# GpSimd's queue takes the stores and fetches of the split weights; SyncE's queue keeps the other transfers

## The chip, the core and the metric

The kernel runs on one core of a Trainium2 chip. A core has five engines that run their own instruction streams in order: TensorE (PE in the profile, with its weight loads shown apart as PEld), VectorE (DVE), ScalarE (ACT), GpSimd (POOL) and SyncE (SP). Transfers between the chip's memory (DRAM) and the core's on-chip memory are carried by 16 DMA engines; a transfer is started by an instruction on the queue of some engine, and an instruction that has to wait for something holds back all that stand behind it on that queue. The metric is the device time of one execution in microseconds; lower is better. A difference of about 0.3% is what a measurement of this kernel can tell from no change.

## What is computed

One inference step of a one-layer hybrid decoder trunk in float32, for a prompt of 2048 tokens and 8 single-token samples, with width 1024:

```python
h = rmsnorm(x, norm_mix)
p = h @ w_in                                  # 1024 x 3980, one combined projection
y_a = gdn_mixer(p_a, ...)                     # gated DeltaNet, chunks of 64
y_b = rwkv_mixer(p_b, ...)                    # RWKV-7
y_c = hgrn_mixer(p_c, ...)                    # HGRN2
x = x + concat(y_a, y_b, y_c) @ w_out         # 1024 x 1024
h = rmsnorm(x, norm_ffn)
u = silu(h @ w_gate) * (h @ w_up)             # 1024 x 2816, twice
x = x + u @ w_down                            # 2816 x 1024
y = rmsnorm(x, norm_final)
```

Beside `y` for prompt and samples, the new states of the three mixers are returned.

## The kernel before, in words

Activations lie transposed: 128 partitions are 128 channels, the free axis is time. Time is cut into four quarters of 512 columns; the last has 520, since the 8 samples are appended, and is worked on as two pieces of 260. For each quarter the kernel does the input projection (31 tiles of 128 output channels, `proj`), the mixers ("units" of two heads, `gdn`, `rwkv`, `hgrn`), the output projection (`out_proj`) and the feed-forward part (`ffn`). A driver (`Driver`, `emit`) writes the units' vector work out between the big products, and a scheduler then fixes the order of every engine's instructions by a model of their times; all of that is settled when the program is built.

Every big product is made exact enough by splitting both operands in two float32r parts, hi and lo, and adding three matmuls: hi·hi, hi·lo, lo·hi (L377, L378, L379, in `mm3`). `load_w` supplies the weights, 512 columns ("a half" of a weight tile of 1024) at a time:

- In the first quarter (q = 0) it loads the raw weight (L331, 256 KB), ACT copies it to hi (L332), DVE makes lo = raw − hi (L333), and the two parts, side by side in one tile `hl`, are stored to DRAM (L340, 512 KB).
- In the quarters after it the two parts are fetched back into such a tile (L347, 512 KB).
- Once the mixers are through, `late` is set and the tiles come from the mixers' buffers; hi and lo are then fetched apart (L345, 256 KB each), up to four weight tiles ahead (`stream`, `AHEAD`). The store at L338 is the same for a late first quarter, which does not occur.

There are four `hl` tiles. So a fetch waits until PE has ended with the half that was fetched four halves earlier, and a split in the first quarter waits until the older store from that tile has landed. The raw weights have three buffers for `w_in` (names `rw_in`) and two for the others (`rw_o`, `rw_wg`, `rw_wu`, `rw_wd`). In the trace, `w_in`, `w_o`, `w_wg`, `w_wu`, `w_wd` are the `hl` tiles, `sw_...` their copies in DRAM, and `hw_...`, `lw_...` the late parts.

Nearly all transfers are issued from SyncE's queue, in the scheduler's order: the weights, the x pieces (`raw_x`, L405), the projected rows (`s_p`, stored at L485 and L489, read back at L497), the mixers' inverses through DRAM (L666 to L694), their results (`s_mix`, L759, read back as `mxs`, L529), the residual (`res`, L537) and the outputs. GpSimd has some 40 instructions in all, among them a few memsets at the start, 20 memsets of the few columns that lie before the first quarter's rows (L496, in `slice_p`), 8 memsets of a whole tile in the HGRN units (`att_h`, L1216) and 6 products at the very end (L643). A memset waits until the buffer it writes is free.

Of the kernel before, what the change touches and what calls it, by code (L numbers as in the profile page):

```python
# [91 lines left out]
class Kern:  # L92
# [218 lines left out]
    def load_w(self, src, key, q, n=1024):  # L311


        nc = self.nc
        out = []
        name = "w_" + "_".join(str(k) for k in key) + f"_{q}"
        for i in range(n // 512):
            if self.late:
                hi, lo = (self.T(f"{j}{name}") for j in "hl")
                parts = hi, lo  # L320
            else:
                hl = self.wp.tile([128, 2, 512], F32, tag="hl", name=name, bufs=4)
                hi, lo = parts = hl[:, 0], hl[:, 1]
            hi, lo = hi.bitcast(F32R), lo.bitcast(F32R)
            if q == 0:
                if key[0] == "in":
                    raw = self.R(f"r{name}")[:, 0:512]
                else:
                    raw = self.wp.tile([128, 512], F32, tag="raw", name=f"r{name}", bufs=2)
                with ExitStack() if key[0] == "in" else self.tc.issue_after(self.mark.ins):  # L330
                    nc.sync.dma_start(raw, src[:, 512 * i:512 * i + 512])  # L331
                nc.scalar.activation(hi, raw, AF.Copy)  # L332
                nc.vector.tensor_tensor(lo, raw, hi, ALU.subtract)  # L333
                kept = self.tc.dram_tile([128, 2, 512], F32, name=f"s{name}_{i}")
                self.kept[key, i] = kept
                if self.late:
                    for j in range(2):
                        nc.sync.dma_start(kept[:, j], parts[j])  # L338
                else:
                    nc.sync.dma_start(kept, hl)  # L340
            else:
                kept = self.kept[key, i]
                if self.late:
                    for j in range(2):
                        nc.sync.dma_start(parts[j], kept[:, j])  # L345
                else:
                    nc.sync.dma_start(hl, kept)  # L347
            out.append((hi, lo))
        return out

# [1348 lines left out]
```

## Time and profile before

| | |
|---|---|
| median of 3 runs | 3178.42 us (3172.18 to 3183.83) |
| profiled execution: its own time | 3181.53 us |
| its span, first to last instruction | 3179.7 us |
| mean granted TensorE clock | 0.979 of full speed |
| DVE busy | 2198.8 us (69%) |
| ACT busy | 1197.5 us (38%) |
| POOL busy | 12.5 us (0%) |
| DMA queue of SyncE | 622.93 MB, 61.4% of the 16 DMA engines' span |
| DMA queue of ACT | 1.07 MB, 0.1% |

"Busy" is the time in which an engine works on an instruction; issuing a transfer is not counted as busy. Matmuls are pipelined and their ends are modelled, so that a PE shown as busy need not be at its peak. A wait is put down to what came last by the profile.

### The profile page before, as it was taken

The page shows a single profiled execution, that of the slowest core. Times are in us where ns is not written, and L with a number is a line of the kernel's source. Part 1 is how long each engine was busy: PE and PEld are TensorE (multiplying, and loading weights), DVE is VectorE, ACT ScalarE, POOL GpSimd, SP SyncE. Part 2 cuts the span into 40 slices and gives each one's busy share as a digit, 9 for nine tenths or more (in the row PEclk, how much of TensorE's full clock was granted, in tenths as well). Part 3 has the DMA queues.
Part 4 walks back from the last instruction along what each step waited for, and adds up shares of the span by engine and source line. Part 5 has one row for each costly group of instructions (what it writes and reads, how often), then busy time and mean ns, then how long its engine had stood idle before and what let it go on. Part 6 is the DMA issues. An engine that isn't in the chain of part 4 may idle for free.

```text
span 3179.7 us, 62651 instructions
## 1 busy us (share of the span) xinstructions
PE 3063.7 (96%) x24812; PEld 2445.6 (77%) x24812; DVE 2198.8 (69%) x5424; ACT 1197.5 (38%) x2063; POOL 12.5 (0%) x41
## 2 busy tenths in 40 slices
PE   7999999999998999999999999997999999999998
PEld 5777777778996677767767777775677777999998
DVE  6783676677667878878788688888676674443334
ACT  5442252244225544553445343546342322221002
POOL 0000000000000000000000000000000000000000
PEclk9999999999999999999999999997999999999999
DMA  8887567657766577676765445555454447755552
GB/s 284 282 287 236 176 194 218 197 175 217 206 179 204 191 240 232 219 232 217 255 188 166 157 158 172 174 181 154 153 170 150 155 158 247 257 170 186 190 182 91
DMA packets 387938, 628.00 MB, mean 198 GB/s; under 512 B 172540, under 2 KB 176892, under 8 KB 387644
## 3 DMA queue, kind: packets, MB, share of 16 engines
q1 hardware_dynamic: 386556, 622.93, 61.4%
q8 instruction: 195, 3.19, 0.4%
q10 hardware_dynamic: 1088, 1.07, 0.1%
q14 instruction: 99, 0.81, 0.1%
HBM read 456.77 MB, written 167.14 MB: 196 GB/s over the span
## 4 chain that ended last, share of the span: by engine, by line
PE 72%; DVE 12%; DMA 9%; ACT 4%; issue 2%; SPq 2%; DVEq 0%; ACTq 0%
PE psp L377 5%; PE psp L378 5%; PE psp L379 5%; PE pd L377 5%; PE pd L379 5%; PE pfu L377 5%; PE pd L378 5%; PE pfu L379 5%; PE pfg L377 4%; PE pfu L378 4%; PE pfg L378 4%; PE pfg L379 4%; DMA rw_in<-w 2%; PE pso L379 1%; PE pso L378 1%
## 5 line engine op out<-in xcount | busy, mean ns | idle before, releaser
L377 PE MATMUL psp<-xs,w_in 128*128 128x512 f32 (+1 forms) x1240 | 447.2, 361 | 21.6 <-ACT xs L417 8.9
L378 PE MATMUL psp<-xs,w_in 128*128 128x512 f32 (+1 forms) x1240 | 443.6, 358 | 0.8 <-DVE xs L418 0.8
L379 PE MATMUL psp<-xs,w_in 128*128 128x512 f32 (+1 forms) x1240 | 438.9, 355 | 0.1
L377 PEld LDWEIGHTS psp<-xs,w_in 128*128 128x128 f32 x1240 | 235.2, 190 | 67.8 <-ACT w_in L332 10.3
L378 PEld LDWEIGHTS psp<-xs,w_in 128*128 128x128 f32 x1240 | 235.2, 190 | 35.6 <-DVE xs L418 2.0
L379 PEld LDWEIGHTS psp<-xs,w_in 128*128 128x128 f32 x1240 | 234.7, 189 | 36.1 <-issue 1.3
L606 DVE TENSOR_TENSOR x<-pd,x 128x512 f32<-128x512 f32 (+1 forms) x240 | 138.2, 583 | 109.9 <-PE pd L379 108.2
L377 PE MATMUL pd<-u,w_wd 128*128 128x512 f32 x496 | 202.0, 414 | 10.0 <-DVE x L606 6.7
L378 PE MATMUL pfg<-xhs,w_wg 128*128 128x512 f32 x496 | 202.6, 408 | 3.7 <-DVE xhs L564 3.6
L377 PE MATMUL pfg<-xhs,w_wg 128*128 128x512 f32 x496 | 202.0, 407 | 0.2
L377 PE MATMUL pfu<-xhs,w_wu 128*128 128x512 f32 x496 | 200.5, 404 | 0.5 <-ACT w_wu L332 0.5
L378 PE MATMUL pd<-u,w_wd 128*128 128x512 f32 x496 | 200.4, 405 | 0.0
L379 PE MATMUL pd<-u,w_wd 128*128 128x512 f32 x496 | 199.1, 403 | 0.0
L379 PE MATMUL pfg<-xhs,w_wg 128*128 128x512 f32 x496 | 199.1, 401 | 0.0
L379 PE MATMUL pfu<-xhs,w_wu 128*128 128x512 f32 x496 | 198.9, 401 | 0.0
L378 PE MATMUL pfu<-xhs,w_wu 128*128 128x512 f32 x496 | 198.3, 400 | 0.0
L585 ACT ACTIVATE t<-t 128x512 f32<-128x512 f32 (+1 forms) x110 | 60.0, 546 | 298.0 <-DVE t L584 292.4
L285 ACT ACT_TABLE_LOAD x91 | 116.8, 1283 | 113.1 <-PE pny L512 23.8
L482 DVE TENSOR_TENSOR p<-psp,ri 128x512 f32<-128x512 f32 (+1 forms) x155 | 89.8, 580 | 72.7 <-PE psp L379 71.3
L362 ACT ACTIVATE u<-t 128x512 fp32r<-128x512 f32 (+1 forms) x110 | 60.1, 546 | 210.7 <-DVE t L588 210.5
L377 PEld LDWEIGHTS pd<-u,w_wd 128*128 128x128 f32 x496 | 94.2, 191 | 34.9 <-DVE x L606 3.0
L587 DVE SCALAR_TENSOR_TENSOR t<-pfu,rf 128x512 f32<-128x512 f32 (+1 forms) x110 | 64.1, 583 | 77.8 <-PE pfu L379 74.7
(645 smaller groups left out, 7296.7 us busy)
## 6 DMA issues: line engine op xcount, KB each, us to landing
w_in<-sw_in SPq DMA_DIRECT2D x186, 512.0 KB, 4.2
w_wg<-sw_wg SPq DMA_DIRECT2D x80, 512.0 KB, 3.3
w_wu<-sw_wu SPq DMA_DIRECT2D x80, 512.0 KB, 3.3
w_wd<-sw_wd SPq DMA_DIRECT2D x80, 512.0 KB, 3.8
sw_in<-w_in SPq DMA_DIRECT2D x62, 512.0 KB, 4.4
s_p<-p SPq DMA_DIRECT2D x93, 256.0 KB, 4.0
sw_wg<-w_wg SPq DMA_DIRECT2D x44, 512.0 KB, 2.9
sw_wu<-w_wu SPq DMA_DIRECT2D x44, 512.0 KB, 2.9
```

What stands on the lines that cost most here:

```text
L285: p = self.nc.scalar.preload_act_table_set("natural_log_exp_and_others")
L362: nc.scalar.activation(out[:, 0], src, AF.Copy)
L377: nc.tensor.matmul(ps, lhsT=hi[:, ws], rhs=xs[:, 0, xc], start=start, stop=False)
L378: nc.tensor.matmul(ps, lhsT=hi[:, ws], rhs=xs[:, 1, xc], start=False, stop=False)
L379: nc.tensor.matmul(ps, lhsT=lo[:, ws], rhs=xs[:, 0, xc], start=False, stop=stop)
L482: nc.vector.tensor_tensor(p[:, c0:c0 + cn], ps, rstd[q][:, c0:c0 + cn], ALU.mult)
L585: nc.scalar.activation(t, g, AF.Tanh, scale=0.5)
L587: nc.vector.scalar_tensor_tensor(p, psu, 0.5, r[:, cs], ALU.mult, ALU.mult)
L606: nc.vector.tensor_tensor(x2[d][:, c0:c0 + cn], ps, x2[d][:, c0:c0 + cn], ALU.add)
```

## The change

Four instructions of `load_w`, which stores and fetches the split weights, are issued from GpSimd's queue and no longer from SyncE's. The raw loads (L331) and every other transfer stay on SyncE.

```diff
                 if self.late:
                     for j in range(2):
-                        nc.sync.dma_start(kept[:, j], parts[j])
+                        nc.gpsimd.dma_start(kept[:, j], parts[j])
                 else:
-                    nc.sync.dma_start(kept, hl)
+                    nc.gpsimd.dma_start(kept, hl)
             else:
                 kept = self.kept[key, i]
                 if self.late:
                     for j in range(2):
-                        nc.sync.dma_start(parts[j], kept[:, j])
+                        nc.gpsimd.dma_start(parts[j], kept[:, j])
                 else:
-                    nc.sync.dma_start(hl, kept)
+                    nc.gpsimd.dma_start(hl, kept)
```

In the built program 1012 transfers change queue: 210 stores (L340), 458 fetches of 512 KB (L347) and 344 late fetches of 256 KB (L345). The scheduler places everything anew, so the order on the other engines shifts by some instructions as well.

SyncE's queue at the program's start, before (`sw_in_0_0` and `sw_in_0_1` are the stores of the first weight tile's halves):

```order
L405 DMA raw_x_229<-xT 128x512 x2
L340 DMA sw_in_0_0_214<-w_in_0_209 128x1024
L340 DMA sw_in_0_1_221<-w_in_0_216 128x1024
L405 DMA raw_x_232<-xT 128x512 x2
L331 DMA rw_in_0_285<-w 128x512
L331 DMA rw_in_0_292<-w 128x512
L186 DMA cst<-cst 128x352
```

The same place on SyncE's queue in the changed program:

```order
L405 DMA raw_x_229<-xT 128x512 x2
L405 DMA raw_x_232<-xT 128x512 x2
L331 DMA rw_in_0_285<-w 128x512
L331 DMA rw_in_0_292<-w 128x512
L186 DMA cst<-cst 128x352
```

The two stores, which wait for DVE's split of the first weight, no longer stand ahead of the last two x pieces and of the next raw weights.

GpSimd's queue in the second quarter's input projection, before (memsets alone):

```order
L496 MEMSET p_g_3741 128x3
L496 MEMSET p_g_3930 128x3
L496 MEMSET pkr_4695 128x1
L496 MEMSET prr_4836 128x1
L496 MEMSET pvr_4852 128x1
```

And in the changed program, from the 105th of the weight transfers on:

```order
L347 DMA w_in_1_4703<-sw_in_0_0_1920 128x1024
L496 MEMSET p_g_3930 128x3
L347 DMA w_in_1_4705<-sw_in_0_1_1927 128x1024
L496 MEMSET pkr_4695 128x1
L347 DMA w_in_1_4777<-sw_in_0_0_2038 128x1024
L347 DMA w_in_1_4779<-sw_in_0_1_2045 128x1024
L347 DMA w_in_1_4904<-sw_in_0_0_2135 128x1024
L496 MEMSET prr_4836 128x1
L347 DMA w_in_1_4906<-sw_in_0_1_2142 128x1024
```

The memsets now have weight fetches ahead of them and behind them on one queue; a memset that waits for its buffer holds the fetches behind it.

## Rows read from the trace of the kernel before

**Rows 1.** The page's first part: busy time of an engine, its share of the span, and the number of instructions.

```profile
PE 3063.7 (96%) x24812; PEld 2445.6 (77%) x24812; DVE 2198.8 (69%) x5424; ACT 1197.5 (38%) x2063; POOL 12.5 (0%) x41
```

**Rows 2.** Busy time by stretch (us from the span's start: length, then the busy time and instructions of PE, PEld, DVE, ACT and POOL; the last three columns are the granted TensorE clock, the busy share of the DMA engines and GB/s).

```profile
0.00:200.00 200.00, 174.26 (x1012) 130.32 (x1013) 152.14 (x336) 103.65 (x168) 2.41 (x20) 0.96 0.87 283
300.00:600.00 300.00, 299.26 (x2564) 221.42 (x2563) 195.45 (x517) 97.89 (x161) 1.13 (x7) 1.00 0.64 198
1000.00:1600.00 600.00, 574.93 (x4325) 429.44 (x4323) 483.15 (x1129) 294.15 (x486) 1.05 (x2) 0.98 0.71 229
2000.00:2200.00 200.00, 184.04 (x1455) 137.97 (x1452) 170.24 (x400) 106.68 (x181) 0.00 (x0) 0.94 0.57 171
2800.00:3000.00 200.00, 200.00 (x1673) 200.00 (x1673) 76.07 (x182) 23.95 (x56) 0.00 (x0) 1.00 0.56 182
```

**Rows 3.** What PE waited for, over the whole span: us in total, times, longest us.

```profile
PE psp L377 <- ACT xs L417: 8.9, 2, 8.7
PE psp L377 <- ACT w_in L332: 8.6, 4, 3.2
...
PE pfu L377 <- DVE x L548: 2.8, 1, 2.8
PE psp L377 <- DMA w_in<-sw_in: 2.8, 3, 1.2
```

**Rows 4.** What SyncE's queue (SPq) waited for, over the whole span: us in total, times, longest us.

```profile
SPq L347 <- PE psp L379: 248.1, 106, 8.4
SPq L347 <- PE pfg L379: 185.7, 59, 7.6
...
SPq L340 <- DVE w_wd L333: 65.2, 28, 11.8
SPq L340 <- DVE w_wu L333: 56.1, 22, 6.0
```

**Rows 5.** The chain of work that ended last, in its first 50 us: start, duration, what.

```profile
8.59 7.47 DMA raw_x<-xT
...
25.37 0.54 SPq L340
26.01 4.98 DMA rw_in<-w
```

**Rows 6.** Timeline of SyncE's queue at the start: start, duration, line, transfer, count.

```profile
2.13 3.08 SPq L405 DMA_DIRECT2D raw_x<-xT  x6
5.53 1.26 SPq L340 DMA_DIRECT2D sw_in<-w_in  x2
7.94 1.03 SPq L405 DMA_DIRECT2D raw_x<-xT  x2
```

**Rows 7.** The raw weight loads (L331): who waited for them (us, times), and the time from issue to landing.

```profile
  ACT w_in L332: 63.5, 26
  ACT w_wg L332: 46.8, 19
  ACT w_wu L332: 43.3, 18
  ACT w_wd L332: 32.1, 21
...
DMA to landing us min/median/max: 3.3/4.2/7.7
```

**Rows 8.** The fetches of the split weights: two rows of SyncE's timeline in the second quarter's projection, and, from the view of line L347 between 270 and 700 us, the time from issue to landing.

```profile
288.73 3.94 SPq L347 DMA_DIRECT2D w_in<-sw_in  x2
...
295.13 3.67 SPq L347 DMA_DIRECT2D w_in<-sw_in  x2
...
DMA to landing us min/median/max: 3.1/3.9/6.7
```

**Rows 9.** How long one instruction takes: fetches on SyncE's queue (ns min/median/max, first and last start in us), and GpSimd's products (busy us, mean ns).

```profile
L347 SPq DMA_DIRECT2D w_in<-sw_in x186: 319/320/1262, 235.8 to 956.0; - x186
...
L345 SPq DMA_DIRECT2D lw_wu<-sw_wu x52: 319/320/2213, 2625.3 to 3104.7; - x52
...
L643 POOL TENSOR_TENSOR yy<-yy,ry 128x260 f32<-128x260 f32 x6 | 5.0, 865 | 589.3 <-ACT ry L299 589.3
```

**Rows 10.** When three of GpSimd's memsets became ready (its timeline; in brackets the idle time before), and when SyncE issued the fetches that stand right behind them in the changed program's order (in a row of two, the second).

```profile
396.47 0.10 POOL L496 MEMSET p_g<- 128x3 f32 x1 [60.17 <-issue]
...
416.04 0.10 POOL L496 MEMSET prr<- 128x1 f32 x1 [18.80 <-DVE cv_g L829]
...
581.11 0.53 POOL L1216 MEMSET att_h<- 128x512 f32 x1 [139.36 <-DVE lo_bd_h L273]
...
383.53 3.10 SPq L347 DMA_DIRECT2D w_in<-sw_in  x2
...
408.76 0.34 SPq L347 DMA_DIRECT2D w_in<-sw_in  x1
...
574.28 3.33 SPq L347 DMA_DIRECT2D w_in<-sw_in  x2
```

**Rows 11.** The late fetches (L345): the first and the last kind to start (ns min/median/max, first and last start in us).

```profile
L345 SPq DMA_DIRECT2D hw_wg<-sw_wg x52: 319/382/961, 2622.8 to 3093.6; - x52
...
L345 SPq DMA_DIRECT2D lw_wd<-sw_wd x52: 319/320/1894, 2678.1 to 3127.7; - x52
```

**Rows 12.** Two groups of DVE instructions over 128x512 elements, the second with one input and both ends on-chip (busy us, mean ns).

```profile
L606 DVE TENSOR_TENSOR x<-pd,x 128x512 f32<-128x512 f32 x144 | 97.6, 686 | 41.6 <-PE pd L379 40.2
...
L974 DVE TENSOR_SCALAR a_r<-a_r 128x512 f32<-128x512 f32 x12 | 5.0, 419 | 2.6 <-ACT a_r L973 2.5
```

## The prediction

> **What bounds the kernel now.** I read the shares of the engines first: PE is busy for 3063.7 of 3179.7 us [rows 1], so only 116 us of its time are idle, and whatever the change does to queues must pass through those 116 us or add to them. The table by stretch shows where they lie [rows 2]: 25.7 us in the first 200 us, 25.1 us between 1000 and 1600 (first output projection and feed-forward part), 16.0 us between 2000 and 2200, and almost none between 300 and 600 or 2800 and 3000. The granted clock sits below 1 in the same stretches: 0.96, 0.98 and 0.94 cost another 8, 12 and 12 us of full-speed time, and it is 1.00 where PE has no gaps. Both of the first two stretches are those in which weights are loaded raw, split and stored.
>
> Next the waits. PE itself waits little for weights: 8.6 us for ACT's split of `w_in`, 2.8 us for a fetched half [rows 3]. SyncE's queue stands a great deal: 248.1 us at fetches until a projection has freed the tile, 185.7 us until a gate product has, and 65.2 and 56.1 us at stores until DVE has made lo [rows 4]. All that is queued behind stands with it. The chain that ended last shows this at the start: a raw x piece issued at 8.59 us, then a store's place on SyncE's queue at 25.37 us directly ahead of a raw weight load at 26.01 us [rows 5].
>
> **The change part by part.** *The start.* The stores leave SyncE's queue. The six x pieces are issued by 5.21 us (2.13 + 3.08), the other two at 7.94, behind the two stores [rows 6]: 2.7 us come off the chain. The raw loads after them are no longer queued behind a store. Their landing takes 4.2 us and ACT stands 63.5 us for those of `w_in` [rows 7]; PE's gaps from it are 8.6 us [rows 3]. I count half of these, 4.3 us, because the DMA engines are 87% busy here [rows 2] and a load still shares them with the stores. That removes 7.0 of 25.7 us of gaps, and I give the clock the same share of its 8 us, 2.2. Together −9.2 us; the bounds are 0 (the raw buffers or the DMA engines set the pace) and −34 (all gaps and all of the clock).
>
> *The first output projection and feed-forward part.* ACT stands 122.2 us for `w_wg`, `w_wu` and `w_wd` [rows 7], and with ACT's queue the activations that stand behind. The idle time and clock are worth 25.1 + 12 = 37.1 us [rows 2]; few of PE's gaps are due to weights directly. I take a quarter: −9.3 us, between 0 and −37.
>
> *The other transfers of SyncE.* Freed from the waits at fetches, the residual and the first fetches of a stage start sooner. PE's gaps for these are 2.8 + 2.8 us [rows 3]; half is −2.8 us. The gaps between 2000 and 2200, 16 us and 12 us of clock, I leave to the range.
>
> *Issuing from GpSimd.* The trace shows no transfer issued there, so the cost is bounded from rows: 0.32 us, SyncE's median, and 2.21 us, the longest that one issue took [rows 9]. I take 0.87 us, what GpSimd's own instruction over 128 partitions takes [rows 9], 0.55 more than now. Cover: two halves are fetched per 6.4 us (288.73 to 295.13) [rows 8], so with four tiles a freed tile is needed again 3 × 3.2 = 9.6 us later; the fetch lands after 3.9 us, at worst 6.7 [rows 8]. Of the 2.9 us that remain at worst, 0.55 is taken, and 1.89 at the upper bound: cost 0. In the late part 344 fetches run between 2622.8 and 3127.7 us [rows 11], one per 1.47 us. At 0.87 GpSimd keeps up: cost 0. At 2.21 it would not: 344 × 0.74 = 255 us.
>
> The Trainium skill, "DMA: Bandwidth & Descriptors", section "Specifications", puts the first byte of a GpSimd-issued transfer at about 1 us and of a SyncE-issued one at about 0.6 us. By that the sum is the same, since 0.4 us more is within the cover.
>
> *Memsets among the fetches.* GpSimd's memsets now hold fetches behind them. In the trace before, the `p_g` memset was ready at 396.47 us, while the fetch right behind it in the new order was issued at 386.3 (383.53 + 3.10 − 0.32): 10.2 us late. The next two such pairs are 416.04 against 408.76, 7.3 us, and 581.11 against 577.3, 3.8 us [rows 10]. The cover is 9.6 − 3.9 − 0.55 = 5.1 us, so 5.1 and 2.2 us reach PE: +7.3 us, between 0 (the scheduler's new order makes the buffers free earlier) and +21.3 (no cover).
>
> *The order drawn anew.* PE's gaps outside the three stretches are 116 − 66.8 = 49 us, mostly ends of DVE and ACT work that came late by the fixed order. A new order can do better or worse; I take 0, with half of it, 25 us, either way.
>
> The sum: −9.2 − 9.3 − 2.8 + 7.3 = −14.0 us. The profiled execution took 3181.5 us, so 3167.5; it stands 3.1 us above the median of the runs, 3178.4, and from the median the forecast is **3164 us**, 0.44% faster.
>
> **The rivals.** *No change that can be told.* The fetches' waits on SyncE are waits for PE itself, and PE's direct loss to weights is 11.4 us in all [rows 3]. If the raw loads are paced by their two or three buffers and by DMA engines that are 87% busy, two queues move the same bytes at the same pace; the gains shrink to a third (−7) and the memsets' +7 cancels them: 3178 us. Against it: the store's place is on the chain [rows 5].
>
> The Trainium skill, "DMA: Bandwidth & Descriptors", section "Issuing engines are not separate DMA queues", speaks for this rival: transfers from all engines end on the same 16 DMA engines, and a second issuing engine saves only the time of issuing. By that rule alone the time stays near 3178 us; the trace agrees so far as issuing costs SyncE only 0.32 us, but it does not show what standing in line costs.
>
> *Slower: weights held on GpSimd.* Place: the last 14 of the 28 memsets of L496 and L1216, which stand among fetches and feed-forward stores. Point: a memset whose buffer is freed more than 5.1 us after the fetch behind it could go, that is, where DVE runs that far behind PE. Price: if all are as late as the worst row, 14 × 5.1 = 71 us; with the gains, 3178 − 21 + 71 = 3228 us. For it: one of the three pairs is that late; against it, the other two have a cost of 2.2 and 0.
>
> *Slower: GpSimd is the bound of the late part.* Point: 1.47 us per issue. At 1.7 us it costs 344 × 0.23 = 79 us, with the other terms 3178 − 14 + 79 = 3243 us; at 2.21, 3419 us. PE has no gap there to hide it in [rows 2]. For it speaks only that no row shows the price.
>
> The Trainium skill, "SBUF — State Buffer", section "SBUF: two separate sides", gives a mechanism: GpSimd writes the descriptors, and is locked out while DVE runs a one-input operation in its double-rate mode; it advises the other queues. The trace has such operations: 0.419 us against 0.686 us for a two-input one [rows 12]. A wait of 0.42 us on top of 0.87 stays under 1.47, so by this rule the sum here stands, but with less room.
>
> **How the numbers follow.** Forecast, faster by more than 0.3% (9.5 us): 0.44, with a range of its own of 3128 to 3168. No change: 0.24. Weights held on GpSimd: 0.20. Late part bound by GpSimd: 0.12. So faster 0.44, same 0.24, slower 0.32. Low end 3128: half of the bounds of the first two terms and of the 2000 to 2200 stretch, (34 + 37 + 28) / 2 = 50 us under the median. High end 3235: past the first slower rival and short of the second; I leave about 0.1 above and 0.1 below.
>
> **What would show it.** Right: the last two x pieces issued by about 6 us; ACT's wait for raw weights well below 63.5 and 122.2 us; PE's idle time under 20 us in the first 200 us and the clock above 0.96 there; no PE waits for L347's tiles beyond some 10 us; late fetches on GpSimd at under 1.47 us each with PE without gaps. Wrong: PE waiting for `w_in`, `w_wg` or `hw_`/`lw_` transfers behind GpSimd's memsets or issues; a late part longer than 505 us; ACT's wait for raw weights unchanged, which would make it no change; or gaps before products of the mixers that grow by more than 25 us, which would be the new order's doing.

## The result, and the profile after

The changed kernel takes 3196.02 us (median of 5 runs, 3192.87 to 3199.32) against 3176.81 for the kernel before beside it: 1.0057 times as long, 95% interval 1.0043 to 1.0072. That is 19 us slower; 3164 us and a gain were forecast. One kernel's executions differ among themselves: the kernel before took between 3162.0 and 3180.4 us in 23 runs on one chip. So a comparison of two single traces carries some 10 us either way, and verdicts below rest on ratios of runs side by side.

The first part of the page and its DMA queues, after:

```profile
PE 3057.3 (96%) x24812; PEld 2443.4 (77%) x24812; DVE 2196.0 (69%) x5424; ACT 1197.5 (37%) x2064; POOL 558.6 (17%) x1053
...
q0 software_dynamic: 123712, 440.47, 40.4%
q1 hardware_dynamic: 240828, 182.46, 20.5%
```

PE works no longer than before [rows 1], within a span of 3193.4 us in place of 3179.7: it is idle for 136.1 us in place of 116.0. The change does what it says: 440 MB have moved to GpSimd's queue (q0). The table by stretch tells where the idle time lies (columns as in [rows 2]):

```profile
0.00:200.00 200.00, 170.82 (x988) 126.97 (x989) 149.00 (x325) 105.20 (x168) 28.70 (x69) 0.94 0.85 278
300.00:600.00 300.00, 292.99 (x2476) 216.69 (x2475) 193.76 (x514) 97.45 (x158) 41.65 (x82) 0.99 0.65 193
1000.00:1600.00 600.00, 566.31 (x4358) 424.68 (x4358) 482.77 (x1138) 290.32 (x485) 84.27 (x158) 0.98 0.68 228
2000.00:2200.00 200.00, 187.01 (x1403) 141.24 (x1403) 156.46 (x370) 93.46 (x155) 25.41 (x47) 0.96 0.55 171
2200.00:2600.00 400.00, 384.07 (x3225) 284.82 (x3225) 294.88 (x754) 146.40 (x249) 53.15 (x98) 0.95 0.50 156
2800.00:3000.00 200.00, 200.00 (x1674) 200.00 (x1673) 77.02 (x181) 28.83 (x61) 74.71 (x138) 1.00 0.56 185
```

The same view of the kernel before has, for the one stretch that [rows 2] leave out:

```profile
2200.00:2600.00 400.00, 392.20 (x3201) 290.91 (x3202) 287.95 (x746) 143.83 (x236) 1.05 (x2) 0.97 0.50 158
```

Length minus PE's busy time, before and after: 25.7 and 29.2 us in the first 200 us, 0.7 and 7.0 from 300 to 600, 25.1 and 33.7 from 1000 to 1600, 7.8 and 15.9 from 2200 to 2600. These are stretches in which mixers run; in another of them, 2000 to 2200, the gaps shrank from 16.0 to 13.0 us. Where none runs, from 2800 to 3000, PE has no gap after as before.

What PE waits for (us in total, times, longest us), the first rows and the only two with a DMA, after:

```profile
PE psp L377 <- ACT w_in L332: 10.8, 5, 4.3
PE psp L377 <- ACT xs L417: 8.4, 1, 8.4
PE pKV_r L1097 <- DVE kt_r L747: 7.9, 2, 6.0
PE px_r L1119 <- DVE Z_r L1134: 6.5, 5, 1.9
...
PE oss_h L274 <- ACT hi_oss_h L272: 5.6, 3, 3.1
...
PE ptv_h L739 <- DMA v_h<-s_p: 1.6, 1, 1.6
...
PE pj_g L710 <- DMA rw_wu<-wu: 1.5, 1, 1.5
```

There is no row for a fetched half, which had 2.8 us before [rows 3]. The new waits end with DVE's and ACT's work for the mixers. Summed over the trace, PE stands idle for 59.1 us before the mixers' products in the kernel before and for 82.6 us after; before all other products it is 47.3 and 44.1 us. What feeds that work are the mixers' transfers, which are still SyncE's. The eight loads of 8 KB that end each inverse's trip through DRAM (L694), first before, then after: who waited for them (us, times), and the time from issue to landing.

```profile
  DVE uT_g L698: 11.5, 6
  DVE uT_r L698: 9.1, 6
...
DMA to landing us min/median/max: 1.6/2.1/5.3
```

```profile
  DVE uT_r L698: 20.8, 8
  DVE uT_g L698: 20.4, 8
...
DMA to landing us min/median/max: 1.7/3.4/6.5
```

They land 1.3 us later in the median, and DVE waits twice as long for them. The trace tells the landing for only a part of the 192 loads (70 before, 25 after). A measure that all 24 inverses have is the time from the store of `inU` (L689), whose data these loads bring back, to the transpose of `inD` (L698) that waits for them: 10.8 us in the mean before, 11.9 after. This became theory A: with a queue of their own, the weights' transfers run beside the mixers' small ones, which land later. Its rival, theory B: the scheduler drew a new order for all engines, and that order made the gaps.

### The profile page after: what moved, and what is told of

Its sections match the earlier page's. It is cut to its first block, busy times and chain, and to the rows that moved or that the text cites. A ratio compares the mean times of both kernels' runs of the same rounds, so it can differ in the third digit from the quotient of the medians.

```text
span 3193.4 us, 62995 instructions
## 1 busy us (share of the span) xinstructions
PE 3057.3 (96%) x24812; PEld 2443.4 (77%) x24812; DVE 2196.0 (69%) x5424; ACT 1197.5 (37%) x2064; POOL 558.6 (17%) x1053
## 4 chain that ended last, share of the span: by engine, by line
PE 70%; DVE 12%; DMA 11%; ACT 4%; issue 2%; SPq 1%; DVEq 0%; ACTq 0%
PE psp L377 5%; PE psp L378 5%; PE psp L379 5%; PE pd L377 4%; PE pd L378 4%; PE pfu L377 4%; PE pfu L379 4%; PE pfu L378 4%; PE pd L379 4%; PE pfg L377 4%; PE pfg L379 4%; PE pfg L378 4%; DMA rw_wg<-wg 1%; PE pso L377 1%; PE pso L378 1%
## 5 line engine op out<-in xcount | busy, mean ns | idle before, releaser
L377 PE MATMUL psp<-xs,w_in 128*128 128x512 f32 (+1 forms) x1240 | 447.8, 361 | 20.9 <-ACT w_in L332 10.8
L347 POOL DMA_DIRECT2D w_in<-sw_in x186 | 100.2, 539 | 626.5 <-PE psp L379 580.8
```

The source lines that it names most:

```text
L347: nc.gpsimd.dma_start(hl, kept)
L377: nc.tensor.matmul(ps, lhsT=hi[:, ws], rhs=xs[:, 0, xc], start=start, stop=False)
```

## The experiments

### The queue and the order taken apart

The order of one kernel can be forced on another: its program is built first, the order of each engine's instructions read from it, and every instruction of the real one chained to its predecessor by an edge that sets the order of issue and waits for nothing.

```diff
+    other = traced(arrays, ('sync', 'sync'))
+    pins = [(i.name, str(i.engine)) for f in other.m.functions for b in f.blocks for i in b.instructions
...
+            for name, e in pins:
...
+                if e in last:
+                    tc.add_manual_dep(i, last[e], mybir.DependencyInfo(
+                        mybir.DependencyClass.NoSync, mybir.DependencyReason.DATA), reason="pin")
+                last[e] = name
```

In e1, e3 and e4 the order is that of the kernel before, in e2 that of the changed kernel; a transfer that changes its queue finds its own place there. The chaining itself costs nothing that shows: e13 below is chained in the same way and takes 0.9989.

> The weights' stores and fetches are issued by GpSimd as in the changed kernel, but TensorE, VectorE, ScalarE and SyncE's other transfers stand in the order of the kernel before. Theory A (the second queue lets the weights' packets run beside the mixers' small transfers, which land later): as slow as the changed kernel, ratio 1.003 to 1.009, and the small transfers land 1 to 2 us later than before (inD 3 us or more against 2.2 and 1.9). Theory B (the scheduler's new order made the new gaps; the queue itself is a small gain): ratio 0.994 to 1.001, gaps of TensorE at or under 116 us, although the small transfers still land late.

> All transfers are issued by SyncE as before, but TensorE, VectorE and ScalarE work in the order of the changed kernel. Theory A: about as fast as the kernel before, ratio 0.998 to 1.003. Theory B: as slow as the changed kernel or slower, ratio 1.004 to 1.015, with TensorE's gaps before the mixers' products at some 115 us as in the changed kernel.

> GpSimd issues the stores of the weights' two parts alone, SyncE the fetches; all engines in the order of the kernel before. The prediction's terms for the start and for the first output projection and feed-forward part (-9.2 and -9.3 us) would stand here alone: ratio about 0.994. Theory A: the stores run beside the mixers of the first 500 us only, so between 0 and a third of the loss, ratio 0.998 to 1.002. Theory B: the same as e1 for those stretches, 0.996 to 1.000.

> GpSimd issues the fetches of the weights' two parts alone, SyncE the stores; all engines in the order of the kernel before. Theory A: most of the loss, ratio 1.003 to 1.007, with the inverse's transfers landing late between 300 and 2600 us. Theory B: ratio 0.996 to 1.001.

| | queue of the stores, fetches | order | ratio to before | 95% interval |
|---|---|---|---|---|
| the change | GpSimd, GpSimd | its own | 1.0057 | 1.0043 to 1.0072 |
| e1 | GpSimd, GpSimd | before's | 1.0082 | 1.0066 to 1.0097 |
| e2 | SyncE, SyncE | the change's | 1.0104 | 1.0091 to 1.0117 |
| e3 | GpSimd, SyncE | before's | 0.9976 | 0.9967 to 0.9985 |
| e4 | SyncE, GpSimd | before's | 1.0088 | 1.0073 to 1.0102 |

Theory A holds for the loss: at the old order the new queue costs 0.82%, and of the two parts only the fetches cost (0.88%, e4), while the stores gain 0.24% (e3). Theory B holds on the old queue alone: there the new order costs 1.04% by itself. The two don't add up: with the queue that it was drawn for, the new order is no worse than the old one (1.0057 against 1.0082, with intervals that overlap).

The stretches 1000 to 1600 and 2200 to 2600 us show where each makes gaps; first e5, a second trace of the kernel before (below), then e4, then e2:

```profile
1000.00:1600.00 600.00, 581.27 (x4469) 435.44 (x4468) 494.04 (x1153) 299.99 (x498) 1.05 (x2) 0.98 0.71 234
2200.00:2600.00 400.00, 393.13 (x3337) 295.00 (x3336) 284.55 (x732) 136.03 (x222) 1.05 (x2) 1.00 0.48 159
```

```profile
1000.00:1600.00 600.00, 577.97 (x4392) 432.50 (x4391) 488.44 (x1137) 297.22 (x489) 6.87 (x13) 0.98 0.70 231
2200.00:2600.00 400.00, 383.25 (x3101) 282.56 (x3101) 281.21 (x728) 144.09 (x236) 52.75 (x100) 0.95 0.47 154
```

```profile
1000.00:1600.00 600.00, 565.96 (x4236) 423.14 (x4235) 477.28 (x1115) 287.96 (x479) 1.05 (x2) 0.97 0.68 226
2200.00:2600.00 400.00, 386.53 (x3239) 287.21 (x3239) 293.08 (x752) 147.02 (x249) 0.53 (x1) 0.95 0.47 156
```

From 1000 to 1600, with the first output projection and feed-forward part, hardly anything is fetched, and e4's gaps of 22.0 us lie between those of the two traces of the kernel before (18.7 in e5, 25.1 in the first); e2 has 34.0, as the changed kernel has 33.7: these are the order's. From 2200 to 2600 e4's gaps are 16.8 us to e5's 6.9 at the same order: these are the fetches'. The new order makes gaps there too, 13.5 us in e2, without them. Read the clock with them: it is 0.95 in e4, against 1.00 in e5 and 0.97 in the first trace of the kernel before, and PE got through 3101 matmuls there and not 3337 (e5) or 3201.

Over the whole span, PE's idle time before the mixers' products is 59.1 and 50.2 us in the two traces of the kernel before, 69.2 in e4 and 73.9 in e1; before all other products it is 47.3, 44.4, 43.6 and 43.2. So the fetches' queue makes its gaps before the mixers' products. The new order alone (e2) makes them before both: 66.7 us before the mixers' products, 59.7 before the others.

The small loads tell that the landing follows the queue and not the order. L694 in e4, then in e2:

```profile
DMA to landing us min/median/max: 1.6/2.9/5.3
```

```profile
DMA to landing us min/median/max: 1.5/1.8/3.9
```

It is 2.0 us in e3 and e5. From the store of `inU` to the transpose it is 10.6 us in e5 and e2, 11.2 in e4 and 11.5 in e1.

The DMA packets of the traces show that the queue had kept the fetches apart from the small transfers. From 1600 to 2600 us every packet of 4 KB is a fetch's, and over that stretch 5.7 to 6.1 of the 16 DMA engines carry one in the mean of any of these traces. In the 2.5 us after the issue of one of the 171 small transfers of the inverses there, it is 3.1 of 16 in e5 and 3.2 in e2, with the fetches on SyncE, but 6.9 in e4 and in e1 and 7.1 in the changed kernel, with the fetches on GpSimd.

### A second trace, and stores alone in an order of their own

> The kernel before once more, unchanged, for a trace from the same chip as the runs beside it. Every theory: the same time as the kernel before, and the inverse's small transfers at 2 us from issue to landing.

One run of 3159.78 us, with a span of 3158.0, 21.7 us shorter than in the first trace of the same program. It lies 2 us under the spread told above, as the first trace lies 1 us over it, and is the trace beside which those of the experiments are set.

> GpSimd issues the stores alone, SyncE the fetches, and the scheduler draws the order anew for it. By e3 the stores' queue is worth 0.24% at the old order; if a new order by itself only costs or gains by chance (theory B), the ratio lies anywhere from 0.99 to 1.01; if an order drawn for its own queue is at least as good as a foreign one (as in the changed kernel against e1), 0.994 to 0.998.

```diff
-                        nc.sync.dma_start(kept[:, j], parts[j])
+                        nc.gpsimd.dma_start(kept[:, j], parts[j])
...
-                    nc.sync.dma_start(kept, hl)
+                    nc.gpsimd.dma_start(kept, hl)
```

1.0063 (1.0050 to 1.0075), outside the range that was expected of an order drawn for its own queue. The same queues at the old order gave 0.9976: the order costs 0.87% here.

### What a later transfer costs

> All transfers on SyncE and the order of the kernel before; the eight 8 KB loads that end each inverse's round trip are issued twice, so each of the 24 inverses has its result some 2.6 to 3 us later (8 more issues of 0.32 us), about what the later landing of four small transfers in a row adds in e4. If the fetches on GpSimd cost by the late small transfers of the inverses alone: ratio 1.006 to 1.010. If the inverses have slack and the loss comes from elsewhere (the mixers' large loads, the fetches themselves): 0.999 to 1.003.

```diff
+        for again in range(2):
             for n in range(4):
                 for b in range(2):
                     o = 32 * n + B * b
                     nc.sync.dma_start(D[o:o + B, :, B * b:B * b + B], su[b, n].rearrange("c j i -> j c i"))
```

1.0270 (1.0257 to 1.0283), three times what was expected. The round trip of an inverse can be read from the timelines, from the first store of N (L666) to the transpose of inD (L698). One of the 24, in e5 and in e4:

```profile
1795.51 1.80 SPq L666 DMA_DIRECT2D s_nr<-N_r  x4
...
1828.84 0.44 DVE L698 STREAM_TRANSPOSE uT_r<-inD 128x256 f32<-128x256 f32 x1
```

```profile
1814.01 1.97 SPq L666 DMA_DIRECT2D s_nr<-N_r  x4
...
1849.24 0.45 DVE L698 STREAM_TRANSPOSE uT_r<-inD 128x256 f32<-128x256 f32 x1 [1.82 <-DMA inD<-s_ur]
```

33.3 us in e5, 35.2 in e4. The mean over the 24 is 39.0 us in e5, 40.6 in e4, 41.2 in e1, 41.9 in the changed kernel and 43.4 in e7. So e7 made the trips 24 × 4.4 = 106 us longer in all and lost 0.0270 × 3170 = 86 us: 0.8 us for a microsecond. In e4, 24 × 1.6 = 38 us cost 0.0088 × 3170 = 28 us: 0.7; in e1, 24 × 2.2 = 53 us cost 26: 0.5. These prices are rough, since the first trace of the kernel before has a mean of 39.6 us: against it, e4's is 1.2. The dose in e7 was larger than I had taken; the price is of the same size. But e7 also gives SyncE 192 more issues, which at the 0.43 us of L694's median take 82 us of its time, as much as was lost.

> The control for e7: the four 8 KB loads of inF are issued three times in place of once, again 192 more issues of SyncE and the same bytes, but for a tile that is needed only some 30 us later; order of the kernel before. If e7 lost by the round trip: 0.999 to 1.006. If it lost by SyncE's time: 1.02 or more.

```diff
+        for again in range(2):
+            for n in range(4):
+                nc.sync.dma_start(F[32 * n:32 * n + B, :, B:], sn[n, :, 0:B, B:].rearrange("c j i -> j c i"))
```

1.0199 (1.0179 to 1.0219). As a control it failed: the round trip was not left alone but grew to 42.1 us, all of it between the first product of `inT` and the store of `inU`. There DVE stood idle for 5.2 us a trip, from 2.2 in e5, by the profile mostly for ACT and PE; that SyncE, held by the repeated loads, had brought these their data late is likely but not shown. 24 × 3.1 = 74 us cost 63: 0.8 to 0.9. So it can't tell SyncE's time from the round trip: both e7 and e15 fit either.

> GpSimd issues only the fetches of the last part (264 to 344 of 256 KB, where no inverse runs any more), SyncE all else; order of the kernel before. If the fetches on GpSimd cost by the inverses' round trip: no loss, 0.998 to 1.002. If they cost by themselves (issue, landing, the shared engines): a part of the 0.88% of e4 by their share of its bytes, 85 of 330 MB, so 1.002 or more.

0.9989 (0.9980 to 0.9999): 344 fetches on GpSimd, with no inverse beside them, cost nothing. So neither the issuing nor the fetches by themselves cost time in this part, which leaves the loss of e4 to the fetches of 512 KB, most of which are issued while mixers run.

### Small transfers beside a stream

> None of the reference is computed; SyncE sends a chain of 32 KB stores and 8 KB loads of the inverse's shapes, each after the one before has landed, in six phases: alone (A), beside 512 KB fetches issued by GpSimd, one in flight (B) or two (C), beside the same fetches issued by ScalarE, one (D) or two (E), and with the fetches issued by SyncE between them (F). Theory A1 (packets of any second queue delay them): alone about 2 us, B and D alike at some 3 us, C and E longer and alike. Theory A2 (it is the software queue): B and C about 3 us or more, D and E near the 2 us of A. Behind a fetch on their own queue (F) they wait for the fetch, 3 us or more.

None of the reference is computed here. The medians over a phase say little, since the streams of C, D and E end before the chain does; read the timeline where the stream runs. From a store `sn` to the next is the round trip of two transfers, in phases A, B, D and F:

```profile
70.01 0.30 SPq L57 DMA_DIRECT2D snA<-N  x1
71.53 0.30 SPq L60 DMA_DIRECT2D inA<-snA  x1
73.06 0.30 SPq L57 DMA_DIRECT2D snA<-N  x1
...
152.81 0.30 SPq L57 DMA_DIRECT2D snB<-N  x1
154.38 0.30 SPq L60 DMA_DIRECT2D inB<-snB  x1
157.01 0.30 SPq L57 DMA_DIRECT2D snB<-N  x1
...
364.59 0.30 SPq L57 DMA_DIRECT2D snD<-N  x1
367.95 0.30 SPq L60 DMA_DIRECT2D inD<-snD  x1
371.24 0.30 SPq L57 DMA_DIRECT2D snD<-N  x1
...
604.12 0.43 SPq L47 DMA_DIRECT2D wF<-wg  x1
605.36 0.30 SPq L57 DMA_DIRECT2D snF<-N  x1
607.75 0.30 SPq L60 DMA_DIRECT2D inF<-snF  x1
608.09 0.43 SPq L47 DMA_DIRECT2D wF<-wg  x1
```

Alone 3.05 us; beside GpSimd's fetches, one in flight, 4.2; beside ScalarE's, one in flight, 6.65; with a fetch ahead of each pair on their own queue 4.0 (604.12 to 608.09). With two in flight, the means while the stream runs are 6.9 us for GpSimd (206.55 to 302.99, 14 pairs) and 8.5 for ScalarE (454.74 to 531.29, 9 pairs). So small transfers land later beside either other queue: it is not GpSimd's way of issuing (A2). That B and D would be alike was wrong: one fetch is issued per 4.15 us in B, per 3.3 in D, per 2.3 in C and per 2.1 in E. Counted by fetches for each pair, the times fall into line whatever the queue: none 3.05 us (A), one 4.0 and 4.2 (F on its own queue, B), two 6.65 (D), three 6.9 (C), four 8.5 (E). A second queue is not slower by itself; it lets more fetches run beside a pair.

### Small transfers on two queues, and a version that beats both

> The weights stay on SyncE and the order is that of the kernel before; of each inverse's small transfers, two of the four stores of N, the four loads of inF and four of the eight loads of inD are issued by GpSimd. The other half of the issues of 0.3 to 0.5 us is gone from SyncE's part of the round trip, which took 39.0 us in the mean of 24 (e5). If the round trip of the inverse is what the change lengthened (41.2 us in e1, and e7 lost 0.8 us for each us of round trip), it is 1 to 2 us shorter here, and the ratio 0.987 to 0.995. If the small transfers pass from one queue to the other with a delay, or only the shared DMA engines matter, the round trip stays at 39 us or more: 0.998 to 1.006.

> e9 with the stores of the weights' parts on GpSimd as in e3; order of the kernel before. If both gains stand side by side: 0.24% below e9. If the small transfers on GpSimd stand in line behind stores that wait for VectorE: in the first 600 us and from 1000 to 1600 the round trip is longer, and the ratio at or over that of e9.

```diff
-            nc.sync.dma_start(sn[n].rearrange("c j i -> j c i"), N[quad(h, jb), :, 32 * jb:32 * jb + 32])
+            (nc.gpsimd if n % 2 else nc.sync).dma_start(sn[n].rearrange("c j i -> j c i"), N[quad(h, jb), :, 32 * jb:32 * jb + 32])
...
-            nc.sync.dma_start(F[32 * n:32 * n + B, :, B:], sn[n, :, 0:B, B:].rearrange("c j i -> j c i"))
+            nc.gpsimd.dma_start(F[32 * n:32 * n + B, :, B:], sn[n, :, 0:B, B:].rearrange("c j i -> j c i"))
...
-                nc.sync.dma_start(D[o:o + B, :, B * b:B * b + B], su[b, n].rearrange("c j i -> j c i"))
+                (nc.gpsimd if b else nc.sync).dma_start(D[o:o + B, :, B * b:B * b + B], su[b, n].rearrange("c j i -> j c i"))
```

e9 gave 0.9965 (0.9952 to 0.9977), e10 0.9946 (0.9932 to 0.9959). The expectation of e9 missed: the round trip stayed at 39.1 us, and while SyncE has fewer issues in a row, the loads land later (L694 3.0 us in the median, from 2.0). What gained the 0.35% was not the round trip; that SyncE has 24 × (2 + 4 + 4) = 240 fewer small issues, or where its other transfers now stand, was not tried apart. e10, with the stores of e3 added, gains what e3 gained on top: it is 0.54% faster than the kernel before, the fastest of this study, with a round trip of 39.5 us: its gain is not in the round trip either.

### How much any redrawn order costs

> The kernel before with four loads of constants at the start (cst, w2a2 twice, g2) issued by GpSimd, nothing else; the scheduler draws the order anew (about half as many lines of TensorE's order differ as for the stores). Theory B (a redrawn order costs or gains by itself): outside 0.997 to 1.003, either way. Otherwise 0.998 to 1.002.

> The kernel before with the five transfers of the samples' buffers (cbuf, pbuf, o_cs, o_smp, o_tail) issued by GpSimd, nothing else; the order is drawn anew. Theory B: outside 0.997 to 1.003, either way, and another value than e11. Otherwise 0.998 to 1.002.

> All transfers on SyncE, the engines in the order that the scheduler drew for e6. If that order is worse by itself: 1.005 to 1.010, with TensorE's gaps between 300 and 600 us at some 5 us and between 2200 and 2600 at some 10 us as in e6. If it is worse only together with stores on GpSimd: 0.998 to 1.002.

```diff
-        nc.sync.dma_start(self.cst, io["cst"])
+        nc.gpsimd.dma_start(self.cst, io["cst"])
```

(e11; the three other loads, and the five transfers of e12, in the same way.) e11: 1.0019 (1.0008 to 1.0029). e12: 1.0002 (0.9993 to 1.0011). e14: 1.0094 (1.0080 to 1.0109). The small edits redraw part of the order for 0 to 0.2%, less than theory B asked of them. The order drawn for the stores costs 0.94% on the old queue and 0.87% on its own (1.0063 to 0.9976): it is worse by itself. That of e2 is worse only without the queue it was drawn for. What in these orders costs the time was not found.

## Why the prediction was wrong, step by step

- **The other transfers of SyncE** (−2.8 us) is the step that failed. Freed from the waits at fetches, they were to start sooner; at the old order the mixers' small ones land later, because twice as many fetch packets run beside them (6.9 of 16 engines in e4, 3.1 in e5, from 1600 to 2600 us), which the common queue had kept apart. Moving the fetches cost 28 us (e4), and no term of the sum held a loss by it. The waits of [rows 4] were read only as time lost to all behind; that they also space the fetches was left out.
- **The order drawn anew** (0, with 25 us either way) was not at fault in the changed kernel, where the new order is no worse than the old (e1), but its bound was too small: on the old queue it costs 0.0104 × 3170 = 33 us (e2). The list of what would show it wrong had named gaps before the mixers' products that grow by more than 25 us and put them down to the order. They grew by 23.5 us (59.1 to 82.6), and 14.8 of these are there at the old order (73.9 in e1).
- **The start** (−9.2) and **the first output projection and feed-forward part** (−9.3) had the right sign for the stores and less than half the size: together 0.0024 × 3170 = 7.6 us in e3, of 18.5. In the changed kernel the signs that I gave for them are met in part:

```profile
2.13 4.44 SPq L405 DMA_DIRECT2D raw_x<-xT  x8
```

```profile
  ACT w_in L332: 44.1, 17
  ACT w_wg L332: 42.8, 20
  ACT w_wd L332: 36.4, 16
  ACT w_wu L332: 34.7, 19
```

  All x pieces are issued by 6.6 us [rows 6], and ACT waits 44.1 us for `w_in`, from 63.5, and 113.9 in the later part, from 122.2 [rows 7]. Yet PE's idle time in the first 200 us is 29.2 us, not under 20, and the clock 0.94. SyncE now stands for the raw buffers, as the no-change rival had it: at L331 until DVE has made lo, a wait that the trace of before doesn't have. The waits at the stores (65.2 us for `w_wd` at L340 [rows 4]) have moved to the raw loads more than they have gone. Two of the rows, after:

```profile
SPq L331 <- DVE w_wd L333: 56.9, 25, 5.8
SPq L331 <- DVE w_wg L333: 54.0, 21, 5.4
```

- **Issuing from GpSimd** (0) was right, and the price below the one taken. The rows that answer to [rows 9] and [rows 11], after:

```profile
L347 POOL DMA_DIRECT2D w_in<-sw_in x186: 537/537/675, 241.1 to 979.4; - x186
...
L345 POOL DMA_DIRECT2D hw_wg<-sw_wg x52: 546/546/555, 2642.0 to 3108.3; - x52
...
L345 POOL DMA_DIRECT2D lw_wd<-sw_wd x52: 546/546/548, 2700.1 to 3142.2; - x52
```

  0.54 us, not 0.87, and far below the 1.47 at which GpSimd would bound the late part; that rival fell. The longest in these rows is 0.68 us, and of all fetches 0.82 us (`w_o`), so a long wait for DVE does not show either. A fetch lands 3.9 us after its issue in the median of L347, within the cover.
- **Memsets among the fetches** (+7.3) came to nothing that shows: no PE wait for a fetched half, and the eight large memsets waited 19.8 us in all (14.8 + 3.1 + 1.9). The rival that was slower by them had the right sign for a wrong reason.
- **The range**, 3128 to 3235, holds the result only because its upper end was set by the two slower rivals, neither of which came true; that is luck. The chances had put 0.32 on slower.

The rule that I set beside the no-change rival, from the Trainium skill, "DMA: Bandwidth & Descriptors", section "Issuing engines are not separate DMA queues", says that transfers from all engines interleave on the same 16 DMA engines. e8 agrees, with 4.2 and 6.65 us for 3.05. The section's second half, that another issuing engine only saves time of issuing, does not hold here: by the issuing there was little to lose or gain (e13), and e4 is 0.88% slower.

What stays open: which of the mixers' transfers cost most (the round trip fits the loss at 0.5 to 1.2 us for a microsecond, but no run delayed it and nothing else, and large transfers share the engines too), and why the scheduler's orders differ by a per cent.

## What to carry to other kernels

A queue that stands waiting is also a gate: before moving the large transfers off it, look at what they will run beside, and price a later landing of the small transfers on the longest chain, not only the free queue. Move first those that run beside nothing critical (here the fetches after the last inverse, which cost nothing), and measure the parts apart: the stores gained at the old order, though they run beside some of the inverses too. Where a scheduler draws the order, measure an edit once at the old order and once at the new, since an order alone can cost more than the edit.

## What the hardware showed that I had not expected

- A chain of one 32 KB store and one 8 KB load takes 3.05 us alone, 4.2 to 6.9 us beside 512 KB fetches issued by GpSimd and 6.65 to 8.5 beside ScalarE's, the longer the more fetches are issued in its time, though the DMA engines are at most 80% busy (e8, its phase E from 455 to 525 us):

```profile
455.00:525.00 70.00, 0.00 (x0) 0.00 (x0) 1.00 0.80 254
```

- In a kernel whose PE is busy for 96% of the span, fetches moved to a second queue cost 28 us though PE waited for none of them: the mixers' small transfers landed about 1 us later (L694, from 2.0 to 2.9 us in the median), the gaps came before the mixers' products, and the granted clock was lower with them (0.97 and 1.00 in the two traces of the kernel before, 0.95 in e4, from 2200 to 2600 us).
